# One encoder layer on one core: the block products' sums go through ScalarE copies and accumulating DMAs, and the last product gets four more seven-product places

## The chip, the cores and the metric

The kernel runs on one core of a Trainium2 chip. A core has TensorE (PE, with a separate row PEld for loading its stationary operand), VectorE (DVE), ScalarE (ACT), GpSimd (POOL), SyncE (SP) and 16 DMA engines. The metric is device time in microseconds of one execution; a difference of about 0.2% is the least that a measurement of this kernel can tell from no change.

## What is computed

One encoder layer on 256 tokens of width 2048, in float32: an input projection, two groups of heads, an output projection, and a gated feed-forward part. The change is in the feed-forward part alone.

```python
h = rmsnorm(x, norm_mix_w)
p = h @ w_in                                  # 8 parts of 1024 columns
mixed = concat(hgrn2(p[:5]), diff_attention(p[5:]))
x = x + mixed @ w_out
h = rmsnorm(x, norm_ffn_w)
u = silu(h @ w_gate) * (h @ w_up)             # 2048 -> 5632
x = x + u @ w_down                            # 5632 -> 2048
```

## The kernel before

**Matmuls.** Each float32 operand is split into a high and a low part (float32r), and each product of a 128x128 block of activations with a 128x512 block of weights is three matmuls: high x high (L772), high x low (L773), low x high (L774). `Stream` brings the weights: a DMA from SP loads a piece `raw` of 128 x 2 x 512 floats (L99), ScalarE casts it to `whi` (L134), VectorE subtracts to get `wlo` (L135). The pieces are split some units ahead of their use; a stall of VectorE or ScalarE reaches TensorE only when that lead is used up.

**Feed-forward.** Weight matrices are worked on in pairs (gate with up, two column blocks of down). `pair_product` goes over steps `i`, one for each pair of 128-row blocks. A *plain* step takes one piece for each matrix and makes 2 x 4 products, 24 matmuls. A *seven* step makes the same 2x2 block products with seven products, in the manner of Strassen and Winograd: it needs four sums of activation blocks (`sums_of`, `split_sums`, four additions, two casts and two subtractions), sums of weight blocks (L127, L128, L131, L132, and split pieces `unit`, `last`, `first sums`, `second sums`), 21 matmuls, and four extra accumulators in PSUM, `m1`, `m5`, `m6`, `m7`, which `fold` adds up after the last seven step of a pair. `S_UP` and `S_DOWN` list the steps that are seven steps. There are 11 up pairs (`f`), in two phases of 6 and 5, and after each phase two down pairs (`cp`); `up` has 8 steps in a pair, `down` 12 in phase 0 and 10 in phase 1. All four blocks of the step take turns up to the last seven step; behind it the first matrix's remaining pieces come first, then the second's.

**Sums after a pair.** `fold` of up: one ScalarE copy of `m1` (L862) and four VectorE additions (L863 to L866). After the pair, `u` and `v` get the plain accumulators (L870, L873), SiLU and product. `fold` of down: a ScalarE copy (L890) and eight VectorE additions (L888) into the residual `xsb`; then L903 adds the plain accumulators, and in the last phase L905 writes the result out.

**Where the feed-forward part begins.** The output projection ends with transposes of the residual on TensorE, `tpx` (L702, with the identity matrix `ident`), from which ScalarE and VectorE make `h2_hi` and `h2_lo` (L706, L707). Then `mixctx.close()` gives the memory of the pools `mixp` and `work` free, and the pool `ffn` is laid over it. `put_sums` makes the activation sums of the two seven steps of up: `r` (L813), `s` (L719 to L722), `hs_hi` and `hs_lo` (L727, L728).

**Order.** The program is written in one order, and a scheduler sets each engine's own order from it. Every engine runs its instructions strictly in that order, and an instruction that waits holds up all behind it.

Of the kernel before, what the change touches and what calls it, by code (L numbers as in the profile page):

```python
# [11 lines left out]
F32 = mybir.dt.float32  # L12
F32R = mybir.dt.float32r
BF16 = mybir.dt.bfloat16
U8 = mybir.dt.uint8
AF = mybir.ActivationFunctionType
ALU = mybir.AluOpType
# [3 lines left out]
P = 128  # L21
SEQ = 256
TT = SEQ // P
NC = 512
# [11 lines left out]
HL_MORE = 2  # L36
PHASES = 2
S_UP = (2, 4)
S_DOWN = ((1, 3, 5, 7), (1, 3, 5))
EVERY_IN, EVERY_OUT, EVERY_FFN, WIDTH = 1, 1, 2, 2  # L40
LB_FLOOR = 1e-30
LB_CEIL = 1.0 - 1e-6
LEVELS = [1, 2, 4, 8, 16, 32, 64]
# [8 lines left out]
def encoder_layer(ctx: ExitStack, tc: tile.TileContext, xT, xr, w_in, w_out, w_gate, w_up, w_down,  # L52
                  nmix_w, params,
                  dist, masks, out):
    nc = tc.nc
# [11 lines left out]
    const = ctx.enter_context(tc.tile_pool(name="const", bufs=1))  # L67
# [4 lines left out]
    mixp = mixctx.enter_context(tc.tile_pool(name="mixp", bufs=1))  # L72
# [107 lines left out]
    def pair_plan(pick, n, s):  # L180

        steps = []

        def unit(c, i):
            srcs.append(pick(c, i))
            return len(srcs) - 1

        for i in range(max(s) + 1):
            if i in s:
                u, v = unit(0, i), unit(1, i)  # L190
                items.extend((("unit", u), ("last", v), ("first sums", u, v), ("second sums", u, v)))
                steps.append(("seven", i))
            else:
                for c in range(2):
                    items.append(("unit", unit(c, i)))
                    steps.append(("plain", i, c))
        for c in range(2):
            for i in range(max(s) + 1, n):
                items.append(("unit", unit(c, i)))
                steps.append(("plain", i, c))  # L200
        return steps

    def half(src, i):
        return halves(src[i // 2])[i % 2]

    phases, up_plan, down_plan = [], {}, {}
    for ph in range(PHASES):
# [4 lines left out]
        for cp in range(NCH_D // 2):  # L212
            down_plan[ph, cp] = pair_plan(lambda c, i: half(w_down[2 * cp + c], 2 * f0 + i),
                                          2 * (f1 - f0), S_DOWN[ph])
    stream = Stream(srcs, items)
# [25 lines left out]
            stream.split(upto)  # L241


    ident = const.tile([P, P], F32, name="ident")
    make_identity(nc, ident)
    nhalf = const.tile([P, 8], F32, name="nhalf")
    nc.gpsimd.memset(nhalf, -0.5)
    dist_sb = const.tile([P, TT, SEQ], F32, name="dist_sb")
    masks_sb = const.tile([P, len(LEVELS), P], U8, name="masks_sb")
    vec = const.tile([P, params.shape[1]], F32, name="vec")  # L250
    nfw = vec[:, 0:NK]
    onw, qnw, kn1, slw = (vec[:, NK + i:NK + i + 1] for i in range(4))
# [426 lines left out]
    for c in range(NCH_D):  # L679
        accs = new_accs()  # L680
        product(m_hi, m_lo, KO1, accs, EVERY_OUT)
        for tt in range(TT):
            xs = xsb[:, tt, c * NC:(c + 1) * NC]
# [5 lines left out]
    for c in range(NCH_D):  # L689
        accs = new_accs()  # L690
        product(m_hi, m_lo, KO2, accs, 0)
        for tt in range(TT):
            xs = xsb[:, tt, c * NC:(c + 1) * NC]
# [3 lines left out]
        for k2 in range(HPC // 2):  # L697
# [6 lines left out]
            for k1 in range(2):  # L704
# [3 lines left out]
                                               in1=h2_hi[:, kk, :].bitcast(F32), op0=ALU.mult, op1=ALU.subtract)  # L708
# [5 lines left out]
    ffn = ctx.enter_context(tc.tile_pool(name="ffn", bufs=2))  # L714
# [15 lines left out]
    class Acts:  # L730
# [13 lines left out]
        def sum(self, i, n):  # L744
            return self.tile(2 * i, 1) if n == 3 else tuple(s[:, self.at[i], n, :] for s in self.s)

    def pair_product(steps, acts, x, m, every, fold):

        todo = []
# [75 lines left out]
    nkp = max(len(p) for p in phases) * HPC  # L825
    n_down = max(len(s) for s in S_DOWN)

    def put_u(f, u, ph, u_hi, u_lo, us_hi, us_lo, ready):
# [10 lines left out]
        yield  # L839
        for j, i in enumerate(S_DOWN[ph]):  # L840
            if 2 * i // HPC * HPC == k0:
# [9 lines left out]
    for ph, fs in enumerate(phases):  # L851
        u_hi, u_lo = (ffn.tile([P, nkp, SEQ], F32R, tag=t, name=t, bufs=1) for t in ("u_hi", "u_lo"))
        us_hi, us_lo = (ffn.tile([P, n_down, 3, P], F32R, tag=t, name=t, bufs=1) for t in ("us_hi", "us_lo"))
        ready = set()
        for f in fs:
            x, m = new_pair_accs()
            u = ffn.tile([P, TT, NC], F32, tag="u", name="u")
            v = ffn.tile([P, TT, NC], F32, tag="v2", name="v", bufs=1)

            def fold():  # L860
                tt = nc.vector.tensor_tensor
                nc.scalar.copy(out=u[:, 0, :], in_=m[0])  # L862
                tt(out=u[:, 1, :], in0=u[:, 0, :], in1=m[2], op=ALU.add)  # L863
                tt(out=v[:, 0, :], in0=u[:, 1, :], in1=m[1], op=ALU.add)
                tt(out=u[:, 1, :], in0=u[:, 1, :], in1=m[3], op=ALU.add)
                tt(out=v[:, 1, :], in0=u[:, 1, :], in1=m[1], op=ALU.add)  # L866

            pair_product(up_plan[f], h_acts, x, m, EVERY_FFN, fold)
            for tt in range(TT):
                nc.vector.tensor_tensor(out=u[:, tt, :], in0=u[:, tt, :], in1=x[0][tt], op=ALU.add)  # L870
                nc.scalar.activation(out=u[:, tt, :], in_=u[:, tt, :], func=AF.Silu, scale=rstd2[:, tt:tt + 1])
            for tt in range(TT):
                nc.vector.tensor_tensor(out=v[:, tt, :], in0=v[:, tt, :], in1=x[1][tt], op=ALU.add)  # L873
                nc.vector.scalar_tensor_tensor(out=u[:, tt, :], in0=v[:, tt, :], scalar=rstd2[:, tt:tt + 1],
                                               in1=u[:, tt, :], op0=ALU.mult, op1=ALU.mult)
            side.append(put_u(f, u, ph, u_hi, u_lo, us_hi, us_lo, ready))

        u_acts = Acts(u_hi, u_lo, us_hi, us_lo, S_DOWN[ph])
        u_acts.ready = ready
        for cp in range(NCH_D // 2):  # L880
            x, m = new_pair_accs()
            xs = [[xsb[:, tt, (2 * cp + c) * NC:(2 * cp + c + 1) * NC] for tt in range(TT)] for c in range(2)]

            def fold():
                t = ffn.tile([P, NC], F32, tag="v2", name="t", bufs=1)

                def add(to, what):
                    nc.vector.tensor_tensor(out=to, in0=to, in1=what, op=ALU.add)  # L888

                nc.scalar.copy(out=t, in_=m[0])  # L890
                add(xs[0][0], t)
                add(t, m[2])
                add(xs[1][0], t)
                add(xs[1][0], m[1])
                add(t, m[3])
                add(xs[0][1], t)
                add(xs[1][1], t)
                add(xs[1][1], m[1])

            pair_product(down_plan[ph, cp], u_acts, x, m, EVERY_FFN, fold)  # L900
            for c in range(2):
                for tt in range(TT):
                    nc.vector.tensor_tensor(out=xs[c][tt], in0=x[c][tt], in1=xs[c][tt], op=ALU.add)  # L903
                    if ph == PHASES - 1:
                        nc.sync.dma_start(out=out[tt * P:(tt + 1) * P, (2 * cp + c) * NC:(2 * cp + c + 1) * NC],  # L905
                                          in_=xs[c][tt])
# [53 lines left out]
```

## Time and profile before

| | us |
|---|---|
| median of 3 runs (lowest to highest) | 1227.65 (1225.65 to 1227.96) |
| the profiled execution | 1226.58 |
| its span in the trace | 1224.5 |
| TensorE busy in the span | 1211.1 (99%) |
| VectorE busy | 985.9 (81%) |
| ScalarE busy | 707.9 (58%) |
| GpSimd busy | 38.0 (3%) |

The profile shows for each engine how long it was busy, what its instructions waited for, and the order of events in time. Matmuls overlap in the pipeline: a matmul's shown duration (389 ns) is longer than the distance from one to the next. An instruction on VectorE or ScalarE also overlaps with the start of the next by some 0.1 us, so that chains are added up by the distances of starts.

### The profile page before, as it was taken

The numbers are of one execution on the slowest core, as the hardware profiler recorded it, in microseconds if no ns is written. First come the engines' busy times: TensorE is split into PE (matmuls) and PEld (weight loads), VectorE is DVE, ScalarE is ACT, GpSimd is POOL, SyncE is SP. The second block draws the span as 40 slices with busy tenths as digits, with TensorE's granted clock in tenths as the row PEclk, the third lists the DMA queues.
The fourth block names the chain that finished last, engine by engine and source line by source line (L and its number), as shares of the span: only waits on it lengthen the run. The fifth ranks groups of instructions, "written<-read, shape, count | busy, mean of one in ns | idle before, by whom it ended". The sixth has DMA issues, their size and how long they took to land.

```text
span 1224.5 us, 15730 instructions
## 1 busy us (share of the span) xinstructions
PE 1211.1 (99%) x5553; PEld 1000.5 (82%) x5553; DVE 985.9 (81%) x1413; ACT 707.9 (58%) x1029; POOL 38.0 (3%) x42
## 2 busy tenths in 40 slices
PE   9999999999999999999999999999999999999998
PEld 6878888887888788878888888888888888888887
DVE  6558977756987776698998988898978989888885
ACT  6657756776775665565554565464545545654542
POOL 0000111000001100000000000000000000000000
PEclk9999999999999999999999999999999999999999
DMA  8965456566445554547666675665657666766763
GB/s 308 314 229 179 150 174 205 189 211 202 149 147 186 190 184 161 188 139 255 240 201 216 227 253 196 222 223 185 216 196 239 203 212 229 253 197 222 232 208 120
DMA packets 79934, 252.51 MB, mean 206 GB/s; under 512 B 8944, under 2 KB 19824, under 8 KB 79856
## 3 DMA queue, kind: packets, MB, share of 16 engines
q1 hardware_dynamic: 79712, 251.52, 61.4%
q8 instruction: 43, 0.70, 0.2%
q14 instruction: 35, 0.29, 0.1%
q10 hardware_dynamic: 144, 0.01, 0.0%
HBM read 238.38 MB, written 13.11 MB: 205 GB/s over the span
## 4 chain that ended last, share of the span: by engine, by line
PE 85%; DMA 6%; DVE 4%; ACT 2%; issue 1%; SPq 1%; POOL 0%; ACTq 0%; DVEq 0%
PE x L773 15%; PE x L774 15%; PE x L772 15%; PE acc L377 9%; PE acc L378 9%; PE acc L376 9%; PE sc L493 2%; PE m L773 2%; PE m L774 2%; PE m L772 2%; DVE wlo L135 2%; DMA zt<-via 2%; DMA raw<-in_w_in 2%; ACT whi L134 1%; DMA ut<-via 1%
## 5 line engine op out<-in xcount | busy, mean ns | idle before, releaser
L134 ACT CAST whi<-raw 128x1024 fp32r<-128x1024 f32 (+1 forms) x497 | 498.2, 1018 | 392.0 <-PE x L774 123.2
L135 DVE TENSOR_TENSOR wlo<-raw,whi 128x1024 fp32r<-128x1024 f32 (+1 forms) x497 | 578.9, 1180 | 156.0 <-ACT whi L134 152.6
L774 PE MATMUL x<-whi,h_lo 128*128 128x512 f32 x594 | 231.2, 389 | 0.0
L773 PE MATMUL x<-wlo,h_hi 128*128 128x512 f32 x594 | 231.1, 389 | 0.0
L772 PE MATMUL x<-whi,h_hi 128*128 128x512 f32 x594 | 220.4, 389 | 0.0
L377 PE MATMUL acc<-wlo,h_hi 128*128 128x512 f32 x512 | 203.2, 397 | 2.9 <-DVE wlo L135 2.9
L378 PE MATMUL acc<-whi,h_lo 128*128 128x512 f32 x512 | 200.4, 393 | 0.0
L376 PE MATMUL acc<-whi,h_hi 128*128 128x512 f32 x512 | 193.5, 399 | 2.6 <-ACT whi L134 2.5
L772 PEld LDWEIGHTS x<-whi,h_hi 128*128 128x128 f32 x594 | 111.5, 188 | 23.3 <-ACT whi L134 0.2
L773 PEld LDWEIGHTS x<-wlo,h_hi 128*128 128x128 f32 x594 | 111.5, 188 | 23.3
L774 PEld LDWEIGHTS x<-whi,h_lo 128*128 128x128 f32 x594 | 111.5, 188 | 23.1
L377 PEld LDWEIGHTS acc<-wlo,h_hi 128*128 128x128 f32 x512 | 96.8, 189 | 24.3 <-DVE wlo L135 6.1
L376 PEld LDWEIGHTS acc<-whi,h_hi 128*128 128x128 f32 x512 | 96.1, 189 | 22.6 <-ACT whi L134 4.2
L378 PEld LDWEIGHTS acc<-whi,h_lo 128*128 128x128 f32 x512 | 96.7, 189 | 19.3
L773 PE MATMUL x<-wlo,u_hi 128*128 128x512 f32 x282 | 109.8, 389 | 0.0
L774 PE MATMUL x<-whi,u_lo 128*128 128x512 f32 x282 | 109.7, 389 | 0.0
L772 PE MATMUL x<-whi,u_hi 128*128 128x512 f32 x282 | 105.1, 390 | 0.4 <-ACT whi L134 0.4
L772 PEld LDWEIGHTS x<-whi,u_hi 128*128 128x128 f32 x282 | 52.6, 188 | 12.4 <-ACT whi L134 1.6
L773 PEld LDWEIGHTS x<-wlo,u_hi 128*128 128x128 f32 x282 | 52.9, 188 | 11.3 <-DVE wlo L135 0.4
L774 PEld LDWEIGHTS x<-whi,u_lo 128*128 128x128 f32 x282 | 52.9, 188 | 10.9
L377 PE MATMUL acc<-wlo,m_hi 128*128 128x512 f32 x128 | 50.2, 393 | 0.5 <-DVE wlo L135 0.5
L378 PE MATMUL acc<-whi,m_lo 128*128 128x512 f32 x128 | 49.9, 390 | 0.0
(192 smaller groups left out, 1289.9 us busy)
## 6 DMA issues: line engine op xcount, KB each, us to landing
raw<-in_w_in SPq DMA_DIRECT2D x127, 512.0 KB, 4.2
raw<-in_w_gate SPq DMA_DIRECT2D x88, 512.0 KB, 4.7
raw<-in_w_up SPq DMA_DIRECT2D x88, 512.0 KB, 4.7
raw<-in_w_down SPq DMA_DIRECT2D x88, 512.0 KB, 4.7
raw<-in_w_out SPq DMA_DIRECT2D x32, 512.0 KB, 4.0
via<-uq SPq DMA_DIRECT2D x44, 128.0 KB, 2.4
ut<-via SPq DMA_DIRECT2D x11, 512.0 KB, 3.3
via<-zq SPq DMA_DIRECT2D x40, 128.0 KB, 3.7
```

Source lines behind the costliest of these rows:

```text
L134: nc.scalar.copy(out=hi[:, k, :], in_=raw[:, k, :])
L135: self.last_split = tt(out=lo[:, k, :], in0=raw[:, k, :], in1=hi[:, k, :].bitcast(F32), op=ALU.subtract)
L376: nc.tensor.matmul(out=acc, lhsT=hi, rhs=whi[:, k, :], start=first, stop=False)
L377: nc.tensor.matmul(out=acc, lhsT=hi, rhs=wlo[:, k, :], start=False, stop=False)
L378: nc.tensor.matmul(out=acc, lhsT=lo, rhs=whi[:, k, :], start=False, stop=last)
L493: nc.tensor.matmul(out=sc[:, j, :], lhsT=kk[:, j * P:(j + 1) * P], rhs=qq(j), start=True, stop=True)
L772: nc.tensor.matmul(out=acc, lhsT=hi, rhs=whi[:, k, :], start=first, stop=False)
L773: nc.tensor.matmul(out=acc, lhsT=hi, rhs=wlo[:, k, :], start=False, stop=False)
L774: nc.tensor.matmul(out=acc, lhsT=lo, rhs=whi[:, k, :], start=False, stop=left[id(acc)] == 0)
```

## The change

`S_DOWN` gets the steps 9 (phase 0) and 7 (phase 1), each for two column pairs: four more seven steps. `us_hi` and `us_lo` grow by it; to make room, `ident`, `dist_sb` and `masks_sb` move from the pool `const`, which lives to the end, to `mixp`, whose memory `ffn` takes over. `fold` of up becomes three ScalarE copies (`m1` to `u`, `m5` twice to `v`), two VectorE additions and two DMAs, issued by GpSimd, that add into `v`. `fold` of down becomes one ScalarE copy, four VectorE additions and four such DMAs that add into `xsb`; L902 and L904 of the changed kernel are L903 and L905 of the one before. The new tiles `t` and `t3` share the two buffers `sm` with `r` and `s`.

```diff
-S_DOWN = ((1, 3, 5, 7), (1, 3, 5))
+S_DOWN = ((1, 3, 5, 7, 9), (1, 3, 5, 7))
...
-    ident = const.tile([P, P], F32, name="ident")
+    ident = mixp.tile([P, P], F32, name="ident")
...
-    dist_sb = const.tile([P, TT, SEQ], F32, name="dist_sb")
-    masks_sb = const.tile([P, len(LEVELS), P], U8, name="masks_sb")
+    dist_sb = mixp.tile([P, TT, SEQ], F32, name="dist_sb")
+    masks_sb = mixp.tile([P, len(LEVELS), P], U8, name="masks_sb")
...
                 tt = nc.vector.tensor_tensor
+                t = ffn.tile([P, NC], F32, tag="sm", name="t")
                 nc.scalar.copy(out=u[:, 0, :], in_=m[0])
-                tt(out=u[:, 1, :], in0=u[:, 0, :], in1=m[2], op=ALU.add)
-                tt(out=v[:, 0, :], in0=u[:, 1, :], in1=m[1], op=ALU.add)
-                tt(out=u[:, 1, :], in0=u[:, 1, :], in1=m[3], op=ALU.add)
-                tt(out=v[:, 1, :], in0=u[:, 1, :], in1=m[1], op=ALU.add)
+                for c in range(2):
+                    nc.scalar.copy(out=v[:, c, :], in_=m[1])
+                tt(out=t, in0=u[:, 0, :], in1=m[2], op=ALU.add)
+                tt(out=u[:, 1, :], in0=t, in1=m[3], op=ALU.add)
+                nc.gpsimd.dma_start(out=v[:, 0, :], in_=t, accum_op=ALU.add)
+                nc.gpsimd.dma_start(out=v[:, 1, :], in_=u[:, 1, :], accum_op=ALU.add)
...
-                t = ffn.tile([P, NC], F32, tag="v2", name="t", bufs=1)
-
-                def add(to, what):
-                    nc.vector.tensor_tensor(out=to, in0=to, in1=what, op=ALU.add)
-
-                nc.scalar.copy(out=t, in_=m[0])
-                add(xs[0][0], t)
-                add(t, m[2])
-                add(xs[1][0], t)
-                add(xs[1][0], m[1])
-                add(t, m[3])
-                add(xs[0][1], t)
-                add(xs[1][1], t)
-                add(xs[1][1], m[1])
+                t = ffn.tile([P, 2, NC], F32, tag="v2", name="t12", bufs=1)
+                t3 = ffn.tile([P, NC], F32, tag="sm", name="t3")
+                tt = nc.vector.tensor_tensor
+                nc.scalar.copy(out=t[:, 0, :], in_=m[0])
+                tt(out=t[:, 1, :], in0=t[:, 0, :], in1=m[2], op=ALU.add)
+                tt(out=t3, in0=t[:, 1, :], in1=m[3], op=ALU.add)
+                for c in range(2):
+                    tt(out=xs[1][c], in0=xs[1][c], in1=m[1], op=ALU.add)
+                for to, what in ((xs[0][0], t[:, 0, :]), (xs[1][0], t[:, 1, :]), (xs[0][1], t3), (xs[1][1], t3)):
+                    nc.gpsimd.dma_start(out=to, in_=what, accum_op=ALU.add)
```

Three places in the order of instructions carry the prediction. The first is VectorE where the feed-forward part begins. Numbers behind names tell buffers apart; `tpx_4767` and `tpx_4776` are transposes of the third column block, `tpx_4829` and `tpx_4838` of the fourth and last; `r_4921`, `s_4922` and `hs_..._4857/4858` are sums of the first seven step. Before:

```order
L135 TENSOR_TENSOR wlo_4912<-raw_4743,whi_4911 128x1024 [waits DMAHW3_49,Activation_49]
L813 TENSOR_TENSOR r_4921<-h2_hi_4596,h2_lo_4597 128x512
L128 TENSOR_TENSOR raw_4805<-raw_4805,raw_4787 128x512 [waits DMAHW4_49,DVE_49]
L707 SCALAR_TENSOR_TENSOR h2_lo_4597<-tpx_4767,vec_176,h2_hi_4596 128x256 [waits Activation_49]
L707 SCALAR_TENSOR_TENSOR h2_lo_4597<-tpx_4776,vec_176,h2_hi_4596 128x256 [waits Activation_49]
L719 TENSOR_TENSOR s_4922<-r_4921 128x128 [waits DVE_49]
L720 TENSOR_TENSOR s_4922<-r_4921 128x128
L135 TENSOR_TENSOR wlo_4939<-raw_4787,whi_4938 128x1024 [waits Activation_49]
L707 SCALAR_TENSOR_TENSOR h2_lo_4597<-tpx_4767,vec_176,h2_hi_4596 128x256 [waits Activation_49]
L721 TENSOR_TENSOR s_4922<-s_4922,r_4921 128x128 [waits DVE_49]
```

After:

```order
L135 TENSOR_TENSOR wlo_4912<-raw_4743,whi_4911 128x1024 [waits DMAHW3_49,Activation_49]
L707 SCALAR_TENSOR_TENSOR h2_lo_4597<-tpx_4767,vec_176,h2_hi_4596 128x256 [waits Activation_49]
L707 SCALAR_TENSOR_TENSOR h2_lo_4597<-tpx_4776,vec_176,h2_hi_4596 128x256 [waits Activation_49]
L135 TENSOR_TENSOR wlo_4939<-raw_4787,whi_4938 128x1024 [waits DMAHW4_49,Activation_49]
L707 SCALAR_TENSOR_TENSOR h2_lo_4597<-tpx_4767,vec_176,h2_hi_4596 128x256 [waits Activation_49]
L707 SCALAR_TENSOR_TENSOR h2_lo_4597<-tpx_4776,vec_176,h2_hi_4596 128x256 [waits Activation_49]
L813 TENSOR_TENSOR r_4921<-h2_hi_4596,h2_lo_4597 128x512 [waits PE_49]
L707 SCALAR_TENSOR_TENSOR h2_lo_4597<-tpx_4829,vec_176,h2_hi_4596 128x256 [waits Activation_49]
L135 TENSOR_TENSOR wlo_4943<-raw_4805,whi_4942 128x512 [waits DMAHW5_49,Activation_49]
L719 TENSOR_TENSOR s_4922<-r_4921 128x128 [waits DVE_49]
L720 TENSOR_TENSOR s_4922<-r_4921 128x128
L707 SCALAR_TENSOR_TENSOR h2_lo_4597<-tpx_4838,vec_176,h2_hi_4596 128x256 [waits Activation_49]
```

`r_4921` stood ahead of most of the third block's instructions and waited for no other engine; now it stands behind them, ahead of the fourth block's, and waits for TensorE, for the last of the transposes `tpx_4838`. The memory of `r` belongs to the pools that `mixctx.close()` gives free, and `ident`, which those transposes read, is now in one of them.

The second place is ScalarE at the same point; `whi_4946` is the cast of the first sums of weights, `whi_4942` of the single block `last`. Before:

```order
L134 CAST whi_4942<-raw_4805 128x512
L134 CAST whi_4911<-raw_4743 128x1024
L706 ACTIVATE h2_hi_4596<-tpx_4767,vec_176 128x256
L706 ACTIVATE h2_hi_4596<-tpx_4776,vec_176 128x256
L134 CAST whi_4938<-raw_4787 128x1024
L706 ACTIVATE h2_hi_4596<-tpx_4767,vec_176 128x256
L706 ACTIVATE h2_hi_4596<-tpx_4776,vec_176 128x256
L134 CAST whi_4946<-raw_4805 128x1024
L727 CAST hs_hi_4857<-s_4922 128x384
L134 CAST whi_4991<-raw_4873 128x1024
```

After:

```order
L706 ACTIVATE h2_hi_4596<-tpx_4829,vec_176 128x256
L134 CAST whi_4942<-raw_4805 128x512
L706 ACTIVATE h2_hi_4596<-tpx_4838,vec_176 128x256
L706 ACTIVATE h2_hi_4596<-tpx_4829,vec_176 128x256
L706 ACTIVATE h2_hi_4596<-tpx_4838,vec_176 128x256
L727 CAST hs_hi_4857<-s_4922 128x384
L134 CAST whi_4946<-raw_4805 128x1024
L134 CAST whi_4991<-raw_4873 128x1024
L134 CAST whi_5000<-raw_4891 128x1024
```

The casts of the fourth block's transposes stood behind `hs_hi` and `whi_4946`, and stand ahead of them now. TensorE's order there is, before:

```order
L702 MATMUL tpx_4838<-ident_167,xsb_88 128x128 x4
L772 MATMUL m5_4868<-whi_4946,hs_hi_4857 128x512
L773 MATMUL m5_4868<-wlo_4947,hs_hi_4857 128x512
L772 MATMUL x00_4863<-whi_4991,h2_hi_4596 128x512
L772 MATMUL x10_4866<-whi_4942,h2_hi_4596 128x512
L773 MATMUL x10_4866<-wlo_4943,h2_hi_4596 128x512
```

After:

```order
L702 MATMUL tpx_4838<-ident_167,xsb_88 128x128 x4
L772 MATMUL m5_4868<-whi_4946,hs_hi_4857 128x512
L772 MATMUL m7_4870<-whi_4946,hs_hi_4857 128x512
L772 MATMUL x00_4863<-whi_4991,h2_hi_4596 128x512
L773 MATMUL m5_4868<-wlo_4947,hs_hi_4857 128x512
L774 MATMUL m5_4868<-whi_4946,hs_lo_4858 128x512
```

In both, the matmul right behind the last transposes needs `whi_4946` and `hs_hi`; the one of `m7` and those of `m5` with the other parts are drawn together.

The third place is VectorE's end of program. Before:

```order
L135 TENSOR_TENSOR wlo_10402<-raw_10330,whi_10401 128x1024 [waits DMAHW0_49,Activation_49]
L888 TENSOR_TENSOR xsb_88<-xsb_88,m5_10111 128x512 [waits DVE_49]
L888 TENSOR_TENSOR t_10359<-t_10359,m7_10113 128x512
L135 TENSOR_TENSOR wlo_10418<-raw_10339,whi_10417 128x1024 [waits DMAHW1_49,Activation_49]
L888 TENSOR_TENSOR xsb_88<-xsb_88,t_10359 128x512 [waits DVE_49]
L888 TENSOR_TENSOR xsb_88<-xsb_88,t_10359 128x512
L135 TENSOR_TENSOR wlo_10434<-raw_10351,whi_10433 128x1024 [waits DMAHW2_49,Activation_49]
L903 TENSOR_TENSOR xsb_88<-x00_10106,xsb_88 128x512 [waits PE_49]
L888 TENSOR_TENSOR xsb_88<-xsb_88,m5_10111 128x512 [waits DVE_49]
L903 TENSOR_TENSOR xsb_88<-x01_10107,xsb_88 128x512 [waits PE_49]
L903 TENSOR_TENSOR xsb_88<-x10_10109,xsb_88 128x512 [waits PE_49]
L903 TENSOR_TENSOR xsb_88<-x11_10110,xsb_88 128x512 [waits DVE_49,PE_49]
```

After:

```order
L135 TENSOR_TENSOR wlo_10494<-raw_10411,whi_10493 128x1024 [waits DMAHW0_49,Activation_49]
L895 TENSOR_TENSOR xsb_88<-xsb_88,m5_10192 128x512 [waits PE_49]
L895 TENSOR_TENSOR xsb_88<-xsb_88,m5_10192 128x512
L135 TENSOR_TENSOR wlo_10504<-raw_10420,whi_10503 128x1024 [waits DMAHW1_49,Activation_49]
L892 TENSOR_TENSOR t12_10513<-t12_10513,m6_10193 128x512 [waits PE_49]
L135 TENSOR_TENSOR wlo_10525<-raw_10478,whi_10524 128x1024 [waits DMAHW2_49,Activation_49]
L893 TENSOR_TENSOR t3_10514<-t12_10513,m7_10194 128x512 [waits DVE_49]
L902 TENSOR_TENSOR xsb_88<-x00_10187,xsb_88 128x512 [waits DMASW2_49,PE_49]
L902 TENSOR_TENSOR xsb_88<-x01_10188,xsb_88 128x512 [waits DMASW4_49,PE_49]
L902 TENSOR_TENSOR xsb_88<-x10_10190,xsb_88 128x512 [waits DMASW3_49,PE_49]
```

Before, the additions of the last `fold` are spread between the last weight splits; now two of them go by DMA, and each of the four last additions waits for one of the four accumulating DMAs (the semaphores `DMASW`) besides TensorE.

## Rows read from the trace of the kernel before

**Rows 1.** The page's busy time, share of the span and instructions of each engine.
```profile
PE 1211.1 (99%) x5553; PEld 1000.5 (82%) x5553; DVE 985.9 (81%) x1413; ACT 707.9 (58%) x1029; POOL 38.0 (3%) x42
```

**Rows 2.** Stretches: length, busy us (count) of PE, PEld, DVE, ACT, POOL; clock, DMA.
```profile
540.00:560.00 20.00, 18.48 (x80) 14.23 (x79) 19.27 (x26) 11.73 (x15) 0.00 (x0) 1.00 0.63 219
```

**Rows 3.** What PE waited for from 480 us on: us in total, times, longest.
```profile
PE m L773 <- DVE wlo L135: 1.1, 2, 0.7
PE m L772 <- ACT whi L134: 0.5, 1, 0.5
PE x L772 <- ACT whi L134: 0.4, 2, 0.2
```

**Rows 4.** Timeline of PE near the end: start us, us, instruction.
```profile
1217.33 0.39 PE L772 MATMUL x<-whi,u_hi 128*128 128x512 f32 x1
...
1219.83 0.39 PE L774 MATMUL x<-whi,u_lo 128*128 128x512 f32 x1
```

**Rows 5.** Groups by shape from 600 us on: count, busy us, mean ns, idle before.
```profile
L135 DVE TENSOR_TENSOR wlo<-raw,whi 128x1024 fp32r<-128x1024 f32 x265 | 318.4, 1221 | 45.3 <-ACT whi L134 43.3
L888 DVE TENSOR_TENSOR t<-t,m 128x512 f32<-128x512 f32 x8 | 5.4, 681 | 0.0
```

**Rows 6.** Timeline of PE where the feed-forward part begins.
```profile
534.19 1.03 PE L702 MATMUL tpx<-ident,xsb 128*128 128x128 f32 x8
534.98 0.48 PE L772 MATMUL m<-whi,hs_hi 128*128 128x512 f32 x1
...
551.55 0.39 PE L773 MATMUL x<-wlo,h_hi 128*128 128x512 f32 x1
```

**Rows 7.** Timeline of DVE in the same stretch.
```profile
526.88 0.69 DVE L813 TENSOR_TENSOR r<-h_hi,h_lo 128x512 f32<-128x512 f32 x1
527.48 0.69 DVE L128 TENSOR_TENSOR raw<-raw 128x512 f32<-128x512 f32 x1
...
529.07 0.28 DVE L720 TENSOR_TENSOR s<-r 128x128 f32<-128x128 f32 x1
529.27 1.22 DVE L135 TENSOR_TENSOR wlo<-raw,whi 128x1024 fp32r<-128x1024 f32 x1
530.40 0.48 DVE L707 SCALAR_TENSOR_TENSOR h_lo<-tpx,vec,h_hi 128x256 fp32r<-128x256 f32 x1
...
546.75 5.76 DVE L135 TENSOR_TENSOR wlo<-raw,whi 128x1024 fp32r<-128x1024 f32 x5
```

**Rows 8.** Timeline of ACT in the same stretch.
```profile
530.31 1.05 ACT L134 CAST whi<-raw 128x1024 fp32r<-128x1024 f32 x1 [0.81 <-PE x L774]
531.26 0.51 ACT L727 CAST hs_hi<-s 128x384 fp32r<-128x384 f32 x1
```

**Rows 9.** PE after a pause in the first part, and a stretch soon after (columns as Rows 2).
```profile
281.13 0.73 PE L376 MATMUL acc<-whi,h_hi 128*128 128x512 f32 x2 [1.63 <-ACT whi L134]
283.00:284.00 1.00, 1.00 (x4) 0.81 (x3) 0.80 (x1) 1.00 (x3) 0.00 (x0) 0.50 0.67 213
```

**Rows 10.** Timelines of DVE and PE at the last up pair's sums and behind them.
```profile
1099.59 0.68 DVE L863 TENSOR_TENSOR u<-u,m 128x512 f32<-128x512 f32 x1
...
1107.26 1.28 DVE L870 TENSOR_TENSOR u<-u,x 128x512 f32<-128x512 f32 x2
...
1110.65 1.23 DVE L135 TENSOR_TENSOR wlo<-raw,whi 128x1024 fp32r<-128x1024 f32 x1 [0.97 <-ACT whi L134]
...
1115.47 0.68 DVE L873 TENSOR_TENSOR v<-v,x 128x512 f32<-128x512 f32 x1
...
1136.01 0.73 PE L772 MATMUL x<-whi,u_hi 128*128 128x512 f32 x2 [0.21 <-ACT whi L134]
```

**Rows 11.** Timeline of ACT: the cast of the last piece of weights.
```profile
1206.65 1.06 ACT L134 CAST whi<-raw 128x1024 fp32r<-128x1024 f32 x1 [1.66 <-PE x L774]
```

**Rows 12.** DMA view of the result's writes (L905, 256 KB each): issue to landing.
```profile
DMA to landing us min/median/max: 2.2/2.6/6.8
```

## The prediction

> **What bounds the kernel now.** I read the busy table first. TensorE is busy 1211.1 of 1224.5 us, 99%, VectorE 81%, ScalarE 58%, GpSimd 3% [rows 1]. Then I took the waits of TensorE for the part of the run that the change touches. From 480 us to the end they come to 2.0 us: 1.1 and 0.5 before matmuls of `m`, 0.4 before `x` [rows 3], nearly all of it in the stretch from 540 to 560, where TensorE is busy 18.48 of 20 us [rows 2]. So the time falls only with matmuls, and rises with each new wait of TensorE that lasts longer than the lead of the split pieces. Near the end eleven matmuls take 2.50 us from start to start, 0.227 each [rows 4].
>
> The profiled execution took 1226.58 us, its span and 2.1 us around it. The median of the runs is 1.07 above that, and I add this at the end. About 0.2%, 2.5 us, is what a measurement can tell from no change.
>
> **Part A, four more seven steps.** Each has 21 matmuls in place of 24: 4 x 3 = 12 fewer, 12 x 0.227 = 2.7 us. TensorE has no other work to put there and almost no waits, so all of it counts: -2.7.
>
> **Part B, the start of the feed-forward part.** This follows from moving `ident`, not from the sums. The order shows that `r` (L813) now waits for the last transposes `tpx_4838`, since its memory was freed by a pool that they still read. Before, `r` ran at 526.88, with no wait for TensorE, and its sums were ready long before the transposes [rows 7]. These start at 534.19 and take 1.03 us, so `r` can start at 535.2 [rows 6]. What follows on VectorE up to the sums that `hs_hi` needs is, in the order after, with distances of starts from [rows 7] (0.60 for 512 columns, 0.20 for 128, 1.13 for 1024; for L707 0.40, its 0.48 less the overlap): `r` 0.60, L707 0.40, the split of 512 columns 0.60, two sums 0.40, two L707 0.80, the weight sum L127 0.60, then L721 with 0.28 to its end. That is 3.7 us, so the sums stand at 538.9. On ScalarE `hs_hi` takes 0.51 and the next cast, `whi_4946`, 1.05 [rows 8]; that cast also waits for L128, which ends at 539.9 by the same count. So `m5`, the first matmul behind the transposes, starts at about 541.0. Before, it started at 534.98 [rows 6]: TensorE stands still for 6.0 us, and by its strict order nothing else can be drawn ahead.
>
> Is that regained? VectorE is late too. From `r` to the split that x00 needs stand 37 instructions: two `r`, four L707, eight sums of 128, four L728, eight weight sums, two splits of 512 and nine of 1024; by the distances above, with 0.35 for an L728, 22.0 us. That ends at 557.3, with up to 0.7 more for waits on ScalarE. Before, TensorE took that split at 551.55 [rows 6], just behind its end (the fourth of the five from 546.75 [rows 7]); so the lag there is 5.9 to 6.6. TensorE has no later waits in which it could catch up. I take +6.4. The lower bound is 4.1: if VectorE has caught up by then, the 2.0 us of waits that the kernel before itself pays fall away and 6.1 - 2.0 is left.
>
> **Part C, the clock.** In the first part TensorE waited 1.63 us at 281.13, and soon after its granted clock was 0.50, 1.2 of 2.4 GHz [rows 9]. The dip lasted some 3 us, of which about half, 1.4 us, is lost. A pause of 6 us may bring the same, but VectorE's lag already covers part of it. Bounds 0 and 1.4; I take +0.5.
>
> **Part D, the accumulating DMAs.** The trace shows no DMA that GpSimd issues and none that adds, so only bounds stand. The result's writes of 256 KB, as large as these, land in 2.2 to 6.8 us, median 2.6 [rows 12]; I take these as the ends. In the last up pair the fold's first add ran at 1099.59 [rows 10]; behind it come now a split of weights and the second add, so that ends about 1102. GpSimd then issues two DMAs; at the mean of its instructions, 38.0 us in 42 [rows 1], 0.9 each, the second is out at about 1104. The add of `u` that waits for the second DMA is the second of the two from 1107.26, and behind it VectorE had two idle gaps of about 1 us, one of them the 0.97 at 1110.65, before the last add of `v` at 1115.47, which waits for TensorE [rows 10]. A landing by 1109.9, within 5.9 us, therefore costs nothing. One of 6.8 delays `u` by 0.9, and TensorE with it at the two phase boundaries, because ScalarE's cast behind the transposed `u` had no reserve there (0.21 us of wait at 1136.01 [rows 10]). In the middle of a phase nothing is lost: the cast of the last piece ran at 1206.65 and was used at 1217.33 [rows 4, 11], and a lead of this size covers a wait of VectorE.
>
> At the end of the program four plain pieces, not eight, now follow the last seven step. The last two DMAs wait for L893, which stands behind the last weight split, some 8.5 us before TensorE's end. Issued one after the other they land between 5 us before that end and 0.3 behind it. I take 0 for D, with 0 to 2.1 as its bounds (0.3 and twice 0.9).
>
> The row shows only that DMAs of this size from SyncE land within that cover [rows 12]. The Trainium skill, "SBUF — State Buffer", in its part on who interferes with whom, speaks against the change: descriptors of a DMA issued by GpSimd are written by GpSimd itself, and while VectorE holds the port pair that they share, these DMAs sit waiting. The page names 2-port copies as the cause; the feed-forward part's VectorE instructions are additions, subtractions and transposes. By the rule for copies D stays 0; if the additions held the port as well, it would be the late rival below. No run here shows which.
>
> **Part E, balance.** The folds lose 22 + 16 additions of VectorE at 0.68 [rows 5], 25.9 us. The new steps add four weight sums, a half split and a split each (some 4.6 us, 18.6 together) and two sets of activation sums (4.0): 3.3 us less in all. ScalarE gets 22 copies more, at about half of a cast's 1.05, and the new steps' casts, some 20 us, at 58% load. Both lie beside TensorE's work: 0.
>
> **Sum:** -2.7 + 6.4 + 0.5 + 0 = +4.2, so 1230.8 on the profiled execution and 1231.9 beside the median. As some of the lag may still be absorbed, I give 1231.5.
>
> **Rivals.** (1) *The lag is partly absorbed.* TensorE loses 6.0 at the transposes, but VectorE recovers by 551 and the old waits vanish: +4.1 - 2.7, without a clock loss +1.4, and with a somewhat shorter chain less; 1228 to 1229.5. For it: VectorE had idle time in this stretch. Against it: it was busy 19.27 of 20 us there [rows 2]. Such a result is a change of around 0.2%, and mostly counts as none. (2) *The DMAs come late.* GpSimd's DMAs are served one behind another, each in over 5 us, so the second lands over 10 us behind the fold, at 1112 or later where 1109.9 is free. `u` is 2 us or more late at both phase boundaries, and the last L902 waits 2 us for the second of its DMAs: +6 or more on top, 1237 and above. It decides from about 4 us for each DMA. (3) *Faster.* The wait of `r` costs nothing, since the semaphore count that it stands for is met by an earlier transpose than the last. Then `r` runs before 535, VectorE keeps its old lead, and part A alone is left: 1227.65 - 2.7 = 1224.9; it decides only if TensorE's pause stays under 0.3 us. Against it: the count answers to the last of the `tpx_4838` matmuls, and behind it two casts follow in series. (4) *The change does not do what it says:* the steps might not be seven steps in the planned order. TensorE's order of the changed kernel, with 12 matmuls fewer, excludes it: 0.
>
> **How the numbers follow.** Forecast 0.66, own range 1229.6 to 1234; rival 1 has 0.18; rival 2 0.11; rival 3 0.05. The range leaves out the upper end of rival 2 and rival 3: 1227.8 to 1236. Slower by over 0.2% is from 1230.1 up: most of the forecast and all of rival 2, 0.73. Within: 0.22, from rival 1 and the lower end of the forecast. Faster: 0.05.
>
> **What would show it.** In the changed kernel's trace: L813 at about 535.2 with TensorE's transposes as what it waited for; behind the last `tpx` a pause of TensorE of about 6 us, released by ScalarE's `hs_hi` or `whi`; a granted clock of 0.50 soon after; 12 matmuls fewer; TensorE's waits from 600 us on under 1 us; the added DMAs landing in 2 to 5 us; VectorE's waits on DMA at L873 under 3 us; the last L902 not held by a DMA. A pause under 3 us, or DMAs over 6.8 us one behind another, would make the prediction wrong.

## The result

| | before | changed |
|---|---|---|
| median (lowest to highest), us | 1226.65 (1225.25 to 1227.96) | 1247.97 (1244.27 to 1249.79) |
| span of the profiled execution | 1224.5 | 1245.9 |

The changed kernel is slower: the ratio is 1.0164, with the interval 1.0141 to 1.0187, that is 17.3 to 22.9 us. The prediction had slower, but 1231.5 with 1227.8 to 1236; the loss is about five times what it gave (17.3 to 22.9 against 1231.5 - 1227.65 = 3.9).

The busy table after the change, in the form of [rows 1]:

```profile
PE 1219.7 (98%) x5541; PEld 997.3 (80%) x5541; DVE 984.3 (79%) x1411; ACT 722.8 (58%) x1063; POOL 71.0 (6%) x80
```

TensorE has 12 matmuls fewer and is busy 8.6 us longer. VectorE has hardly less to do. What TensorE waited for from 480 us on, beside [rows 3] (us in total, times, longest):

```profile
PE m L772 <- ACT whi L134: 8.1, 5, 5.9
PE x L772 <- ACT whi L134: 5.2, 12, 0.9
PE m L773 <- DVE wlo L135: 0.8, 1, 0.8
```

One wait of 5.9 stands there, and twelve of 0.2 to 0.9 before `x`, where the kernel before had two. The long one is at the place that the prediction named. TensorE's timeline there, beside [rows 6]:

```profile
534.99 1.03 PE L702 MATMUL tpx<-ident,xsb 128*128 128x128 f32 x8
541.91 1.19 PE L772 MATMUL m<-whi,hs_hi 128*128 128x512 f32 x2 [5.89 <-ACT whi L134]
```

VectorE's, where `r` stands behind an idle time of 4.49 us that the transposes end:

```profile
536.07 0.69 DVE L813 TENSOR_TENSOR r<-h_hi,h_lo 128x512 f32<-128x512 f32 x1 [4.49 <-PE tpx L702]
```

And the granted clock, in stretches of 1 us (columns as [rows 2]): 0.50, the lower of TensorE's two levels, 1.2 GHz, from the first matmul behind the pause to 547 and through most of the next stretch.

```profile
542.00:543.00 1.00, 1.00 (x3) 0.57 (x3) 1.00 (x2) 1.00 (x2) 0.00 (x0) 0.50 0.00 0
...
546.00:547.00 1.00, 1.00 (x4) 0.81 (x3) 1.00 (x3) 0.21 (x1) 0.00 (x0) 0.50 0.43 107
547.00:548.00 1.00, 1.00 (x4) 0.77 (x3) 1.00 (x2) 0.41 (x1) 0.00 (x0) 0.56 0.89 279
```

What VectorE waited for from 560 us on shows the second loss. The first row is the addition of `x01` into `u`, in all 11 up pairs (L873 here is L870 of the kernel before); the second is the last additions of down pairs.

```profile
DVE u L873 <- DMA v<-u: 31.5, 11, 4.7
...
DVE xsb L902 <- DMA xsb<-t: 11.6, 5, 4.7
```

The issues of the accumulating DMAs (KB each, median us from issue to landing):

```profile
xsb<-t POOLq DMA_DIRECT2D x16, 256.0 KB, 7.7
v<-t POOLq DMA_DIRECT2D x11, 256.0 KB, 7.6
v<-u POOLq DMA_DIRECT2D x11, 256.0 KB, 8.6
```

**A measure for the parts.** Traces of different executions reach the last transposes anywhere between 532 and 539 us, also where the program up to there is the same. I therefore take from each trace the distance from the start of the last `tpx` group to the start of the last matmul. Before it is 1219.83 - 534.19 = 685.6; in the changed kernel 1241.65 - 534.99 = 706.7, or +21.0. What happens ahead of the transposes is not in this measure.

### The profile page after: what moved, and what is told of

It reads as the page before. It is cut to its first block, busy times and chain, and to the rows that moved or that the text cites. A ratio compares the mean times of both kernels' runs of the same rounds, so it can differ in the third digit from the quotient of the medians.

```text
span 1245.9 us, 15848 instructions
## 1 busy us (share of the span) xinstructions
PE 1219.7 (98%) x5541; PEld 997.3 (80%) x5541; DVE 984.3 (79%) x1411; ACT 722.8 (58%) x1063; POOL 71.0 (6%) x80
## 5 line engine op out<-in xcount | busy, mean ns | idle before, releaser
L773 PE MATMUL x<-wlo,u_hi 128*128 128x512 f32 x262 | 102.0, 389 | 0.0
L774 PE MATMUL x<-whi,u_lo 128*128 128x512 f32 x262 | 102.0, 389 | 0.0
L772 PE MATMUL x<-whi,u_hi 128*128 128x512 f32 x262 | 95.6, 391 | 1.5 <-ACT whi L134 1.5
L772 PEld LDWEIGHTS x<-whi,u_hi 128*128 128x128 f32 x262 | 48.9, 188 | 13.0 <-ACT whi L134 3.2
L773 PEld LDWEIGHTS x<-wlo,u_hi 128*128 128x128 f32 x262 | 49.2, 188 | 10.5 <-DVE wlo L135 0.2
L774 PEld LDWEIGHTS x<-whi,u_lo 128*128 128x128 f32 x262 | 49.2, 188 | 10.2
```

What stands on the lines that cost most here:

```text
L772: nc.tensor.matmul(out=acc, lhsT=hi, rhs=whi[:, k, :], start=first, stop=False)
L773: nc.tensor.matmul(out=acc, lhsT=hi, rhs=wlo[:, k, :], start=False, stop=False)
L774: nc.tensor.matmul(out=acc, lhsT=lo, rhs=whi[:, k, :], start=False, stop=left[id(acc)] == 0)
```

## The experiments

The first four kernels take the change apart. The theory: the three parts add up (pause at the transposes +8, matmuls -2.7, DMAs +15). First rival: VectorE's late start explains the later waits too. Second rival: the parts hurt only together.

**Only the tiles moved.**

```diff
-    ident = const.tile([P, P], F32, name="ident")
+    ident = mixp.tile([P, P], F32, name="ident")
...
-    dist_sb = const.tile([P, TT, SEQ], F32, name="dist_sb")
-    masks_sb = const.tile([P, len(LEVELS), P], U8, name="masks_sb")
+    dist_sb = mixp.tile([P, TT, SEQ], F32, name="dist_sb")
+    masks_sb = mixp.tile([P, len(LEVELS), P], U8, name="masks_sb")
```

> The kernel before with ident, dist_sb and masks_sb moved to mixp and nothing else. Theory (three parts that add up): L813 waits for the last transposes, TensorE pauses about 5.9 us at 535, its granted clock is 0.50 for some 6 us after it, and the waits that the kernel before has at 546 to 551 are gone: +7 to +9 us, 1234 to 1236. First rival (the loss comes from the late start, which VectorE never makes up): +15 or more, 1242 and above, with waits of TensorE in every up pair. Second rival (the parts hurt only together): under +4.

Measured: 1.0071 (1.0053 to 1.0090), +8.7 us. TensorE's timeline has the same pause:

```profile
542.66 1.19 PE L772 MATMUL m<-whi,hs_hi 128*128 128x512 f32 x2 [5.88 <-ACT whi L134]
```

The distance behind the transposes is +7.8. In the up pairs TensorE runs as before: the steps from one pair to the next within a phase are 42.16 us, to the hundredth those of the kernel before; only the step across the phase boundary is 0.8 longer. So the late start is not carried on through the pairs, and the first rival falls.

**Only the folds by DMA.**

```diff
+                t = ffn.tile([P, NC], F32, tag="sm", name="t")
                 nc.scalar.copy(out=u[:, 0, :], in_=m[0])
...
+                for c in range(2):
+                    nc.scalar.copy(out=v[:, c, :], in_=m[1])
+                tt(out=t, in0=u[:, 0, :], in1=m[2], op=ALU.add)
+                tt(out=u[:, 1, :], in0=t, in1=m[3], op=ALU.add)
+                nc.gpsimd.dma_start(out=v[:, 0, :], in_=t, accum_op=ALU.add)
+                nc.gpsimd.dma_start(out=v[:, 1, :], in_=u[:, 1, :], accum_op=ALU.add)
...
```

(and down's fold as in the change)

> The kernel before with only the two folds of the changed kernel (ScalarE copies and accumulating DMAs); S_DOWN and the place of ident stay as before. Theory: the DMAs land 7 to 9 us after their issue, VectorE stands 2 to 5 us before L873 in each up pair, u comes late and so does ScalarE's cast behind it; TensorE loses 0.3 to 1 us in each up pair and some at the boundaries and the end: +10 to +16 us, 1237 to 1243. First rival: DMAs alone within +2 us. Second rival: under +5.

Measured: 1.0135 (1.0114 to 1.0155), +16.5 us; the distance behind the transposes is +15.8. There is no pause at the transposes here. So the DMAs alone make three quarters of the loss, and the second rival falls too.

**The change without the DMAs** (its S_DOWN and moved tiles, the folds of before).

> The changed kernel with the folds of the kernel before (ScalarE copy and VectorE additions, no accumulating DMA); four more seven steps and ident in mixp stay. Theory: the pause at 535 with its half clock, +8, and 12 matmuls fewer, -2.7: +4 to +7 us, 1231 to 1234, and from 600 us on TensorE waits under 2 us. First rival: as slow as the changed kernel, +15 and above. Second rival: under +2.

Measured: 1.0070 (1.0048 to 1.0092), +8.6 us, above what was expected; the distance behind the transposes is +5.6, near the 5.1 expected from 7.8 - 2.7. That lies just below the interval of the times (+5.9 to +11.3); the 3 us between the two are taken up below.

**The seven steps alone, with dist_sb and masks_sb moved.**

```diff
-S_DOWN = ((1, 3, 5, 7), (1, 3, 5))
+S_DOWN = ((1, 3, 5, 7, 9), (1, 3, 5, 7))
...
-    dist_sb = const.tile([P, TT, SEQ], F32, name="dist_sb")
-    masks_sb = const.tile([P, len(LEVELS), P], U8, name="masks_sb")
+    dist_sb = mixp.tile([P, TT, SEQ], F32, name="dist_sb")
+    masks_sb = mixp.tile([P, len(LEVELS), P], U8, name="masks_sb")
```

> Only the four more seven steps: folds of the kernel before, ident back in const, dist_sb and masks_sb in mixp for the room. Theory: L813 waits for no transpose, no pause at 535, 12 matmuls fewer: -2 to -3 us, 1223.5 to 1225.5, ahead of both kernels. Rival: VectorE, which keeps its additions and gets 18.6 us of weight sums and splits more, is late in down, TensorE waits there and the gain is gone: 0 to +4 us.

Measured: 0.9993 (0.9982 to 1.0005), -0.9 us. The distance behind the transposes is -2.9. The gain stands in the trace and hardly in the times: open at this point.

The next four look for what in the DMAs costs. The theory: VectorE's wait at the addition into `u` makes `u` late, and all behind it.

**DMAs that copy instead of adding.**

```diff
-                nc.gpsimd.dma_start(out=v[:, 0, :], in_=t, accum_op=ALU.add)
-                nc.gpsimd.dma_start(out=v[:, 1, :], in_=u[:, 1, :], accum_op=ALU.add)
+                nc.gpsimd.dma_start(out=v[:, 0, :], in_=t)
+                nc.gpsimd.dma_start(out=v[:, 1, :], in_=u[:, 1, :])
...
-                    nc.gpsimd.dma_start(out=to, in_=what, accum_op=ALU.add)
+                    nc.gpsimd.dma_start(out=to, in_=what)
```

> The changed kernel with its GpSimd DMAs copying instead of adding (the sums are then left out of the result). It tells what in a DMA takes 8 us. If the reading, adding and writing of the target costs it: landing 2 to 4 us, VectorE's waits at L873 nearly gone, and most of the 15 us from 560 on back. If issuing by GpSimd or the queues full of weights cost it: landing stays at 7 to 9 us, and the time within 2 us of the changed kernel.

Measured: 1.0056 (1.0040 to 1.0072), +6.9 us: within the noise of the change without the DMAs (+8.6), so all of the DMAs' loss is back. The landing went only part of the way down; issues and VectorE's waits from 560 us on:

```profile
xsb<-t POOLq DMA_DIRECT2D x16, 256.0 KB, 5.8
v<-t POOLq DMA_DIRECT2D x11, 256.0 KB, 6.0
v<-u POOLq DMA_DIRECT2D x11, 256.0 KB, 6.3
...
DVE u L873 <- DMA v<-u: 7.5, 8, 2.3
```

By these medians adding costs 1.6 to 2.3 us for each DMA. With landings of 6.0 to 6.3 VectorE still waits, but at most 2.3, and TensorE loses nothing by it: the distance behind the transposes is +4.8, against +5.6 without the DMAs. How much of the landing is the load of weights is taken up at the end of this section.

**Only up's fold by DMA** (folds of up as above, all else as before).

> The kernel before with only up's fold in the new form (22 DMAs); down's fold, S_DOWN and ident as before. Theory (a late u is what costs): +7 to +11 us, 1234 to 1238, with TensorE's waits in the up pairs and at both phase boundaries. Rival (the load of the DMA queues and the sums of down cost): under +4.

Measured: 1.0130 (1.0111 to 1.0150), +15.9 us, more than was expected: the 22 DMAs of up make as much as both folds together.

**Only down's fold by DMA.**

> The kernel before with only down's fold in the new form (16 DMAs). Theory: VectorE waits before L903 at the end of each down pair, which the lead covers in most; +1 to +5 us, with a later end by the last DMAs among them. Rival: +7 or more.

Measured: 0.9999 (0.9983 to 1.0016). Sixteen DMAs of 7.5 us each in the median, and no change that the times resolve (-2.1 to +2.0 us; in the trace, +1.8 behind the transposes).

**Up's second DMA reads a tile of its own** (against the kernel with only up's fold by DMA).

```diff
+                t2 = ffn.tile([P, NC], F32, tag="t2", name="t2", bufs=1)
...
                 tt(out=t, in0=u[:, 0, :], in1=m[2], op=ALU.add)
                 tt(out=u[:, 1, :], in0=t, in1=m[3], op=ALU.add)
+                tt(out=t2, in0=t, in1=m[3], op=ALU.add)
                 nc.gpsimd.dma_start(out=v[:, 0, :], in_=t, accum_op=ALU.add)
-                nc.gpsimd.dma_start(out=v[:, 1, :], in_=u[:, 1, :], accum_op=ALU.add)
+                nc.gpsimd.dma_start(out=v[:, 1, :], in_=t2, accum_op=ALU.add)
```

> As the kernel with up's DMA fold alone, but the second DMA reads a tile of its own (one more addition on VectorE for each pair), so that the addition into u does not wait for the DMA; only the additions into v do, some 7 us later. Theory (VectorE's wait at the addition into u costs): that wait is gone, the v additions wait under 1 us each, and at least half of the loss of up's DMA fold is back: +1 to +4 us. Rival (the late v costs, wherever VectorE waits): the same loss as with up's DMA fold, +7 to +11.

Measured: 1.0009 (0.9995 to 1.0023), +1.1 us, and 0.0 in the distance behind the transposes. The DMAs are as slow as before, and VectorE waits for none of them (its waits on DMAs from 560 us on):

```profile
v<-t POOLq DMA_DIRECT2D x22, 256.0 KB, 7.8
...
DVE s L719 <- DMA ut<-via: 8.1, 7, 1.5
```

The loss of up therefore comes from one wait in each pair: the second DMA reads `u[:, 1, :]`, and the next addition writes there, so it waits until the DMA has landed. The sums in `v` are needed some 7 us later and wait for nothing.

**Both repairs together** (the change with `ident` in const and the DMA's own tile), and the seven steps timed once more beside it.

> The whole change with two repairs: ident back in const, and up's second DMA reads a tile of its own. Theory (the pause at 535 and the wait at the addition into u are all that the change loses): no pause at 535, no wait of VectorE at L873, 12 matmuls fewer; -3 to +1 us, 1222 to 1226. Rival (the DMAs cost more beside the longer down products): +4 or more.

> The four more seven steps alone with ident in const, timed a second time beside the repaired kernel, since the first timing left open whether the 2.7 us of part A arrive. If they do: -2 to -3 us. If VectorE's extra work takes them back: within 1 us of the kernel before.

Measured: the repaired change 1.0009 (0.9994 to 1.0024), with no pause and no wait at the addition into `u`; 19 us are back. The steps alone 1.0002 (0.9990 to 1.0014). In both the -2.7 does not come through in the times; behind the transposes they show -0.8 and -2.6.

**Where the 2.7 are.** First the move of the two tiles alone:

```diff
-    dist_sb = const.tile([P, TT, SEQ], F32, name="dist_sb")
-    masks_sb = const.tile([P, len(LEVELS), P], U8, name="masks_sb")
+    dist_sb = mixp.tile([P, TT, SEQ], F32, name="dist_sb")
+    masks_sb = mixp.tile([P, len(LEVELS), P], U8, name="masks_sb")
```

> The kernel before with dist_sb and masks_sb in mixp and nothing else; ident stays in const. It asks where the 2.7 us of part A are that the traces show behind the last transposes and the timed runs do not. If the move of these two tiles makes the part ahead of the transposes longer: +1.5 to +2.5 us here, with the last transposes at 536 or later. If the first part only scatters from run to run: within 1 us, and the last transposes anywhere from 533.3 to 536.7, as in the other traces.

Measured: 1.0016 (1.0005 to 1.0027), +2.0 us (0.6 to 3.3). The order of instructions is the same on every engine and only addresses differ. The difference is clear of zero by its interval, but below the 0.2% that a measurement can tell from no change. Its trace reaches the last transposes late, at 538.65:

```profile
538.65 1.03 PE L702 MATMUL tpx<-ident,xsb 128*128 128x128 f32 x8
```

Then the four steps with all three tiles left in const; `lprod`, 512 bytes in each partition that are used at the start only, makes the room:

```diff
-S_DOWN = ((1, 3, 5, 7), (1, 3, 5))
+S_DOWN = ((1, 3, 5, 7, 9), (1, 3, 5, 7))
...
-    lprod = const.tile([P, 2, DH], F32, name="lprod")
+    lprod = mixp.tile([P, 2, DH], F32, name="lprod")
```

> The four more seven steps alone: ident, dist_sb and masks_sb all stay in const, and the small tile lprod, which is used only at the start, goes to mixp for the room. If part A is worth its 2.7 us and the move of dist_sb and masks_sb took some 2 of them: -2 to -3.5 us, 1222 to 1224, ahead of both kernels. If part A is worth less in the timed runs than the traces show: within 1 us of the kernel before.

Measured: 0.9971 (0.9959 to 0.9983), -3.6 us (-5.0 to -2.1): **faster than both kernels**, with the waits of the kernel before and no new one (TensorE from 480 us on):

```profile
PE m L773 <- DVE wlo L135: 1.0, 2, 0.7
PE m L772 <- ACT whi L134: 0.5, 1, 0.5
```

Behind the transposes it is 1214.85 - 532.06 = 682.8, -2.8. So part A is worth what it should be. That the moved tiles took some 2 us of it ahead of the transposes fits the times (+2.0 for the move alone; the steps with the move -0.9 and +0.2, without it -3.6), but the traces do not show it: two of those with the same move (the change without DMAs and the repaired one) reach the transposes at 533.3 and 534.6, where the kernel before does at 534.2. What in the move costs is open.

**Who issues.** The kernel before with its eight writes of the result issued by GpSimd.

```diff
-                        nc.sync.dma_start(out=out[tt * P:(tt + 1) * P, (2 * cp + c) * NC:(2 * cp + c + 1) * NC],
+                        nc.gpsimd.dma_start(out=out[tt * P:(tt + 1) * P, (2 * cp + c) * NC:(2 * cp + c + 1) * NC],
```

> The kernel before with its eight writes of the result issued by GpSimd instead of SyncE: same size, same place. If issuing by GpSimd makes a DMA slow: landing 5 to 7 us in place of 2.6, as the copying DMAs of the other run (5.8 to 6.3). If the way from one tile to another makes it: landing stays at 2 to 3.5.

Measured: landing 2.5 us, as SyncE's 2.6 [rows 12]:

```profile
out<-xsb POOLq DMA_DIRECT2D x8, 256.0 KB, 2.5
```

Both medians mix writes at different places. The first two go out at about 1160 us, with pieces of weights still in flight; the last four follow when the last piece has landed. The last four took 2.2 from SyncE and 2.5 from GpSimd, the first two, SyncE's of the kernel before and GpSimd's of this one:

```profile
out<-xsb SPq DMA_DIRECT2D x2, 256.0 KB, 6.8
...
out<-xsb POOLq DMA_DIRECT2D x2, 256.0 KB, 6.0
```

So GpSimd's issuing is not what makes a DMA slow here. The way from one tile to another is not either. The four DMAs of the last fold run with no weights beside them: in the run that copies they are issued from 1212.9 us on and the last piece of weights lands at 1213.3, in the changed kernel from 1228.8 on and at 1229.1. Here they are, first copying, then adding:

```profile
xsb<-t POOLq DMA_DIRECT2D x4, 256.0 KB, 2.3
...
xsb<-t POOLq DMA_DIRECT2D x4, 256.0 KB, 3.3
```

Over the whole run, nearly always beside the weights, such DMAs took 5.8 to 6.3 and 7.6 to 8.6 in the median. In the first copy of these four, 1213.0 to 1215.3, VectorE is as busy as elsewhere (2.09 of 2.30 us), and the DMA engines are busy 0.30 of the time, against 0.93 from 603.7 to 609.7, where a copy took 6.0. So most of the slowness comes with the load of weights on the 16 DMA engines; adding comes on top, some 1.0 us without the weights and 1.6 to 2.3 beside them. This is read from different places of the same traces; no run changes the load by itself.

## Why the prediction was wrong

**What bounds** was right: TensorE, with no reserve of its own.

**Part A, -2.7:** right. The seven steps alone give -3.6 (-5.0 to -2.1), and -2.8 behind the transposes. What the prediction did not have is that the move of two tiles, which made the room for them, seems to take some 2 us of it.

**Part B, +6.4:** right in mechanism, about 1 us too large. L813 ran at 536.07 behind the transposes, 0.9 later than written, and the transposes 0.8 later; TensorE stood still for 5.89 where 6.0 was worked out, and `m5` came 6.1 later against the transposes than before. VectorE's lag did not simply last: by the distances between matmul starts, the waits that the kernel before has at 546 to 551, 2.5 us, fell away, and others of 1.6 us came at 558 to 559. That leaves 5.2, between the prediction's lower bound of 4.1 and its 6.4.

**Part C, +0.5:** too small, and beyond its upper bound of 1.4. The clock stayed at 0.50 from the first matmul at 541.9 to 547.9; 6 us at half speed cost 2.9 us by the distances of starts (2.4 in the trace of the moved tiles, where the matmul comes later in the dip). The loss was taken from a dip behind a pause of 1.6 us, and set low since VectorE's lag should cover it. B and C together are +7.8 in the trace of the moved tiles, against 6.9; that the sum is near is luck, since the two misses nearly cancel.

**Part D, 0 with 0 to 2.1:** this is the step that failed, by 15.8 us. Two things in it were wrong, the landing and above all the cover in the middle of a phase; the count of what is free at the consumer held.

The landing. The nearest row was the writes of the result, 2.2 to 6.8 with a median of 2.6 [rows 12]. Up's accumulating DMAs took 7.6 and 8.6 in the median, beyond its upper end. The row's median is that of writes with few or no weights beside them; the two that go out beside the weights, as up's DMAs do, took 6.8 each, already more than the 5.9 that was free, and adding came on top.

The consumer. The prediction saw that the addition of `u` waits for the second DMA and gave it until 1109.9 in the last pair. VectorE's wait came to 4.7 at most and 2.9 in the mean, which with those landings is what the same count gives (8.6 - 5.9 = 2.7). Copies of 6.0 to 6.3, just past the 5.9, cost TensorE nothing, so the count of what is free held.

The cover, the main miss. The prediction says that in the middle of a phase nothing is lost, since the last piece of weights is cast 10.7 us ahead of its use [rows 4, 11]. That is the lead at the end of the program. In each up pair the transposed `u` returns by DMA, and ScalarE's cast of it stands in ScalarE's order between weight casts, where it already waits in the kernel before. Two rows from before, the cast and the seven step's start on TensorE:

```profile
621.53 1.05 ACT L836 CAST u_hi<-ut 128x1024 fp32r<-128x1024 f32 x1 [2.47 <-DMA ut<-via]
...
622.52 0.84 PE L772 MATMUL m<-whi,hs_hi 128*128 128x512 f32 x3
```

The same chain in one pair of the changed kernel: VectorE's wait at the addition, ScalarE's cast, the seven step, and TensorE's wait for the weights cast behind it:

```profile
660.15 0.69 DVE L873 TENSOR_TENSOR u<-u,x 128x512 f32<-128x512 f32 x1 [2.67 <-DMA v<-u]
...
676.88 1.05 ACT L836 CAST u_hi<-ut 128x1024 fp32r<-128x1024 f32 x1 [2.44 <-DMA ut<-via]
...
676.50 0.84 PE L772 MATMUL m<-whi,hs_hi 128*128 128x512 f32 x3
...
680.29 0.73 PE L772 MATMUL x<-whi,h_hi 128*128 128x512 f32 x2 [0.46 <-ACT whi L134]
```

Before, the cast starts 0.99 ahead of the seven step; now 0.38 behind it, 1.4 later against TensorE, and TensorE waits for the next cast of weights. ScalarE's wait of 2.47 us was in the trace of before, in all eleven pairs (2.2 to 2.5); the prediction read it at the phase boundary only (its 0.21 at 1136.01 [rows 10]) and not in the pairs. From 634.05 to 676.50 us, TensorE's lag behind the kernel before grew by 0.3, and by a further 0.75 up to the pair's second seven step: about 1 us in this pair. Most of that is in waits that the table shows short or not at all: it counts a wait only from the shown end of the matmul before, 389 ns behind its start, where the next start is due after 227 ns.

By the distances of starts, the +15.8 of the kernel with only the folds by DMA are 8.0 in the up pairs within the phases, where the prediction had nothing, 6.6 around the two phase boundaries, where it had 0 to 1.8 by the path that it named, and 1.2 in the last down pair.

The tail, a fear of the second rival, cost little. In the changed kernel's VectorE timeline the second of the last additions waits 2.44 us for a DMA, the last one for TensorE:

```profile
1239.09 0.69 DVE L902 TENSOR_TENSOR xsb<-x,xsb 128x512 f32<-128x512 f32 x1 [2.44 <-DMA xsb<-t]
...
1242.08 0.69 DVE L902 TENSOR_TENSOR xsb<-x,xsb 128x512 f32<-128x512 f32 x1 [0.67 <-PE x L774]
```

**Rivals.** The second, late DMAs, is what happened, with `u` late through the second DMA, but in every pair and not at the boundaries only; it had 0.11. Two things in it were wrong. The DMAs are not served one behind another: the second is issued about 1.7 us behind the first and lands some 2.6 behind it, while each takes 7 to 9. And it does not decide from 4 us each: copies of 6.0 to 6.3 cost nothing. The rule on DMAs issued by GpSimd that stood beside it (the Trainium skill, "SBUF — State Buffer", in its part on who interferes with whom) is not what made them late here. With GpSimd as issuer the two writes beside the weights landed in 5.6 and 6.5 us, against SyncE's 6.8, with VectorE busy 4.53 of the 5.60 us of the first.

**Sum.** By the times, -3.6 for the steps, +8.7 for the three moved tiles and +16.5 for the DMAs are 21.6, within the measured 17.3 to 22.9; behind the transposes, -2.8 + 7.8 + 15.8 = 20.8 against 21.0. The parts add up.

## What to carry to other kernels

A lead is a number of one place: look for the instructions that wait already in the profile, because a delay ahead of those has no cover, however far ahead the others are. A DMA holds what it reads as well as what it writes; with a source that nobody writes soon, DMAs just as slow cost up's fold nothing here. Take the landing time of a DMA from one that goes beside the same load, not from a median over places. And when tiles move to make room, look at which reader frees their memory, and time the move by itself.

## What the runs showed of the hardware

- DMAs of 256 KB beside a stream of weights took 5.8 to 6.3 us in the median as copies from tile to tile, 6.0 and 6.8 as writes to memory (issued by GpSimd and by SyncE), and 7.6 to 8.6 when adding. With the weights landed the same kinds took 2.3, 2.2 to 2.5, and 3.3.
- A pause of 5.9 us left TensorE at 1.2 GHz from its first matmul at 541.9 to 547.9 us, some 2.9 us more; the pause alone is not the whole price.
- With two tiles at other addresses, and the same instructions in the same order, the times were 2.0 us longer (0.6 to 3.3). That is at the edge of what they can tell, and no trace shows a cause.
